# A hybrid encoder layer on one core: weights of the feed-forward in four steps, later gates, and earlier loads for its down projection

## The chip, the cores and the metric

The kernel runs on one core of a Trainium2 chip. The metric is the time of one execution on the device in microseconds (us). The core has a tensor engine (PE) with its weight loads (PEld), a vector engine (DVE), a scalar engine (ACT), GpSimd (POOL) and a queue engine (SP). Each works through its own list of instructions in order, and semaphores hold an instruction until its operands are there. Transfers are issued from SP and POOL and move on their own.

## The reference, cut to what matters

One layer with 1024 positions and a width of 1024, in float32. The change lies in the feed-forward at its end and in the down projection behind it:

```
x  = x + y @ w_out                       # y: the two gated token mixers
h2 = rmsnorm(x, ffn_norm_w)
up = h2 @ ffn_w_up                       # 1024 -> 2 * 2816
gate, val = split(up, 2)
gate = dwconv3(gate, ffn_dw_w) + ffn_dw_b     # along the positions, zero padded
x  = x + (silu(gate) * val) @ ffn_w_down
out = rmsnorm(x, final_norm_w)
```

## The kernel before

Activations lie with channels on the 128 partitions and positions along the free axis, in two halves of 512 positions. Every float32 factor is split into two parts: a high part, which ACT casts to the matmul's reduced type (`A.copy`, line 122), and a low part, which DVE subtracts (line 119). A product then takes three matmuls, high by high, high by low and low by high (`mm3`, lines 144 to 146), each 128x128 by 128x512.

The feed-forward runs over 22 pairs. Pair j makes 128 channels of the gate and 128 of the value, 1024 input channels deep (`ffn_job`, `pair_job`). A pair is a 2x2 block product done with seven block products in place of eight. Products 1, 2, 6, 7, 5, 4 and 3 follow each other on PE; each has four steps of three matmuls, and a job yields after two of those steps, so that a pair has 14 pieces of six matmuls. The weights of the seven products are sums and differences of raw blocks. These sums are made by transfers that add into their target (`G.dma_start(o, a, accum_op=ALU.add)`, line 242), issued from POOL: first the columns `sw` take in the second source, then half of the raw rows `wr` takes in a half of `sw` ("wr<-sw"), then the other half takes in the first ("wr<-wr"). The split of w1 and w2 reads the rows before these adds, the split of w6 and w3 reads them afterwards. w7 and w5 come from `sw` (pages `wq`), w4 from `w4` (page `wq`). There are two buffers for `wr`, one for `sw`, one for `w4`, four pages `wp` (w1/w2 and w6/w3, high and low) and three pages `wq`.

Between the products, ACT copies product 1, the sum after product 6 and product 7 out of PSUM (`copy`, line 270, pages `su`), since product 6 and 5 go on adding in the bank `row`, and product 4 in the bank `col`. DVE forms the four quadrants in `evac` (lines 1278 to 1285). With the last gate quadrant the gate follows: three taps of the convolution (ACT line 1289, then DVE line 1293 twice), Silu (ACT line 1301), times the norm (line 1302), times the value (line 1303), and the store of g to the scratch tensor `d_g` from SP (line 1304), for each half.

The h2 blocks are linear combinations too. Four sets are made while w_out runs (`parts`, with the tile `hx`, and `h7`); the sets for products 4 and 3 are loaded again from scratch (`late_load`, `late_parts`, pages `ft` and `hy`). The norm of h2 is not applied to the activations but to the results: `rstd_over_partitions` sums the squares on PE (line 424), POOL takes the power (lines 408 and 409), and `spread` turns it with PE (line 416) into a row over all partitions (`rs`, line 417).

`run_jobs` prepares a pair's weights when four pieces of the pair before it have been issued; `Stream.fill(n)` issues n pieces. Down (22 blocks of g, in groups of 4, 4, 5, 5 and 4) loads g from `d_g` into `ev` pages (line 1358), splits it into `hx` and `gx` pages, and for each of eight column blocks accumulates a group in PSUM; the first group's results are copied by ACT to `xr` (line 1363), the next groups add there on DVE (line 1369), and the last one adds x2 and goes through the final norm.

The program order is that of the Python code on PE alone (`manual_schedule` for PE). On the other engines, a scheduler at build time orders the instructions by when it takes their operands to be ready. So a cast can stand far ahead of its place in the code.

Of the kernel before, what the change touches and what calls it, by code (L numbers as in the profile page):

```python
# [29 lines left out]
H = 512  # L30
# [15 lines left out]
def tile_hybrid_encoder(  # L46
# [57 lines left out]
    def tmp():  # L104
        return page(mp, "tm", 4)
# [9 lines left out]
        nc.sync.dma_start(t, src)  # L115
        return t

    def split_lo(eng, lo, src, hi):
        eng.tensor_tensor(lo, src, hi.bitcast(F32), op=ALU.subtract)  # L119

    def split(hi, lo, src, eng):
        A.copy(hi, src)  # L122
        split_lo(eng, lo, src, hi)
        return hi, lo

    def w_cols(w, r0, nk, c0, cols=P):
# [12 lines left out]
    def mm3(acc, w, act, k, first, last, again=False):  # L139
# [5 lines left out]
        T.matmul(acc, whi[:, k, :], alo, start=False, stop=False, skip_group_check=again)  # L145
        T.matmul(acc, wlo[:, k, :], ahi, start=False, stop=last, skip_group_check=again)  # L146

    def run_jobs(jobs, lead=0, prime=0):  # L150


        jobs = jobs if isinstance(jobs, collections.deque) else collections.deque(jobs)
        ready = collections.deque()

        def prepare(n):
            while jobs and len(ready) < n:
                prep, run = jobs.popleft()
                ready.append((run, prep()))

        prepare(max(prime, 1))
        if prime:
            yield
        while ready:
            run, w = ready.popleft()
            pieces = run(w)
            for _ in itertools.islice(pieces, lead):
                yield
            prepare(1)
            yield from pieces  # L170
            prepare(1)

    class Stream:
# [48 lines left out]

        return prep, run

    def pair_job(src0, src1, nk, acts, wpool, pool, evac, su=4, first=False):

# [1 line left out]

        def prep():
            def both(src, alt):
                hi, lo = split(w_page(2 * nk, alt), w_page(2 * nk, alt), src, V)
                return [(hi[:, :nk], lo[:, :nk]), (hi[:, nk:], lo[:, nk:])]

            def add(o, a):
                if first:
                    V.tensor_tensor(o, o, a, op=ALU.add)  # L240
                else:
                    G.dma_start(o, a, accum_op=ALU.add)  # L242

            w = {}
# [1026 lines left out]
    def ffn_job(j):  # L1271
        g = gp[j % 2]
        val = [None, None]

        def evac(e, half, x0, x1=None, op=None):
            if e == 1:
                val[half] = page(fu, "ft", 4)
                V.tensor_tensor(val[half], x0, x1, op=op)
                return
            gh = g[:, 1 + half * H : 1 + (half + 1) * H]  # L1280
            if half == 0:
                V.tensor_tensor(gh, x0, x1, op=op)
                return
            V.tensor_tensor(g[:, 1 : 1 + H], g[:, 1 : 1 + H], rstd2[0], op=ALU.mult)
            V.tensor_tensor(gh, x0, rstd2[1], op=ALU.mult)
            for hf in range(2):
                o = hf * H
                c = tmp()
                A.activation(  # L1289
                    c, g[:, o : o + H], AF.Identity, scale=vec("fdw", j), bias=vec("fdb", j)  # L1290
                )
                for k in (1, 2):
                    V.scalar_tensor_tensor(  # L1293
                        c,
                        g[:, o + k : o + k + H],
                        vec("fdw", k * NF + j),
                        c,
                        op0=ALU.mult,
                        op1=ALU.add,
                    )  # L1300
                A.activation(c, c, AF.Silu)
                V.tensor_tensor(c, c, rstd2[hf], op=ALU.mult)
                V.tensor_tensor(val[hf], val[hf], c, op=ALU.mult)
                nc.sync.dma_start(d_g[j][hf], val[hf])

        return pair_job(
            w_cols(ffn_w_up, 0, ND, j * P),
            w_cols(ffn_w_up, 0, ND, DFF + j * P),
            NK2,
            lambda i: h2[i],  # L1310
            fw,
            fu,
            evac,
        )

    s_ffn = Stream(run_jobs([ffn_job(j) for j in range(NF)], 4))
# [4 lines left out]
    s_ffn.fill(5)  # L1321
    rstd2 = [next(st) for st in stats]

    def late_parts(i, src):
        h2[i].append(split(page(fu, "hy", 16, F32R), page(fu, "hy", 16, F32R), src, V))

    def late_load(src):
        t = page(fu, "ft", 4)
        nc.sync.dma_start(t, src)
        return t  # L1330

    for k in range(NK2):
        b21 = late_load(d_t6[k])
        G.dma_start(b21, d_h2[k + NK2][0], accum_op=ALU.add)
        late_parts(4, b21)
    for k in range(NK2):
        late_parts(3, late_load(d_h2[k + NK2][1]))
# [7 lines left out]
    n_g = itertools.cycle([0] * 32 + [1] * 16)  # L1345

# [1 line left out]
        return hx() if next(n_g) == 0 else page(fd, "gx", 16, F32R)  # L1348

    groups = [4, 4, 5, 5, 4]  # L1350
    gs, jobs = [], []

    def load_g(f0, n):
        for f in range(f0, f0 + n):
            gs.append([])
            for half in range(2):
                t = ev()
                nc.sync.dma_start(t, d_g[f][half])
                gs[-1].append(split(g_page(), g_page(), t, V))

    def first_evac(i):
        def f(half, acc):
# [75 lines left out]
    out_sum, out_y = [], []  # L1438
    fnw = fd.tile([P, D], F32, name="fnw")
    f0 = 0  # L1440
    load_g(0, groups[0])
    nc.sync.dma_start(
        fnw, bass.AP(tensor=final_norm_w.tensor, offset=final_norm_w.offset, ap=[[0, P], [1, D]])
    )
    for n, group in enumerate(groups):
        last = n == len(groups) - 1
        for hs in ((0,), (1,)) if last else ((0, 1),):
            st = Stream(run_jobs(down_jobs(f0, group, hs, final_evac if last else add_evac if n else first_evac)))
            st.fill(3)
            while late:  # L1450
                finish(late.pop())
            if not last:
                st.fill(9)
# [3 lines left out]
            st.drain()  # L1457
        f0 += group
    finish(late.pop())
    fd.release()  # L1460
# [32 lines left out]
```

## Time and profile before

| | |
|---|---|
| median of 3 runs | 1862.43 us (1860.35 to 1862.73) |
| profiled execution, its own time | 1861.67 us |
| its span | 1859.9 us |
| granted PE clock, mean | 0.99 |
| DMA queues: from SP, from POOL | 41.5%, 15.2% of 16 engines' span |

The span is the time from the first to the last instruction in the profile; the run's own time has some us around it. "busy" is the time in which an engine works on an instruction; a matmul's end is modelled. In a wait such as "PE mm L144 <- ACT su L270", the tensor engine's matmul of line 144 stood until ACT's instruction of line 270 had written `su`; the numbers are the total, how often, and the longest. In a timeline row, the idle time just before the instruction and what ended it stand in brackets. Rows by stretch give each engine's busy time with its instructions, then the granted clock, the share of busy DMA engines and GB/s. Tiles are called by the program's names without their numbers.

### The profile page before, as it was taken

What the parts mean: (1) busy time and instruction counts of PE and PEld (TensorE: products, weight loads), DVE (VectorE), ACT (ScalarE), POOL (GpSimd) and SP (SyncE); (2) the same over time, 40 slices, a digit from 0 to 9 for tenths busy, and PEclk for the clock granted to TensorE, in tenths of its full rate; (3) what the DMA queues carried; (4) which work ended last, traced back from release to release, by engine and by line L of the source; (5) the groups of instructions that cost most, each with busy time, mean ns of one, the idle gap of its engine ahead of it and who ended that gap; (6) DMA issues with size and microseconds to landing.
All of it is one profiled execution on the core that took longest, in us unless ns stands there. A gap on an engine that the chain in (4) does not pass through costs nothing.

```text
span 1859.9 us, 23747 instructions
## 1 busy us (share of the span) xinstructions
PE 1778.8 (96%) x8574; PEld 1475.4 (79%) x8574; DVE 1275.2 (69%) x1878; ACT 793.9 (43%) x1482; POOL 172.9 (9%) x189
## 2 busy tenths in 40 slices
PE   8989999999999999999989999899999999999996
PEld 6877877887778888888878787677888888788885
DVE  4599999645479999999835565566666767534445
ACT  6443333334555556555442144443343434522124
POOL 1201111111000000000000001211111111000000
PEclk9999999999999999999999999999999999999998
DMA  7657878874753333332238566876676765733135
GB/s 271 215 146 181 180 175 197 198 173 135 222 170 95 109 114 114 110 105 93 73 120 231 182 210 197 177 163 137 149 155 150 151 155 124 218 95 95 56 87 170
DMA packets 324620, 283.51 MB, mean 152 GB/s; under 512 B 14862, under 2 KB 247062, under 8 KB 324502
## 3 DMA queue, kind: packets, MB, share of 16 engines
q1 hardware_dynamic: 273462, 241.10, 41.5%
q0 software_dynamic: 51040, 40.90, 15.2%
q8 instruction: 67, 1.10, 0.2%
q14 instruction: 51, 0.42, 0.1%
HBM read 189.14 MB, written 72.88 MB: 141 GB/s over the span
## 4 chain that ended last, share of the span: by engine, by line
PE 56%; DVE 20%; DMA 13%; ACT 5%; issue 4%; POOL 1%; SPq 0%; DVEq 0%; ACTq 0%; POOLq 0%
PE mm L144 14%; PE mm L145 14%; PE mm L146 13%; DMA tm<-d_a 3%; PE sc L144 3%; PE sc L146 3%; PE sc L145 3%; DVE wp L119 2%; DVE acc L756 2%; DMA wr<-wr 2%; DVE kG L841 2%; DVE DE L841 2%; DVE qF L841 1%; DMA sw<-in_w_in_dram 1%; DMA wr<-sw 1%
## 5 line engine op out<-in xcount | busy, mean ns | idle before, releaser
L144 PE MATMUL mm<-hx,wp 128*128 128x512 f32 x1176 | 477.4, 406 | 19.4 <-DVE ev L541 7.8
L146 PE MATMUL mm<-hx,wp 128*128 128x512 f32 x1176 | 462.5, 393 | 2.9 <-DVE wp L119 2.9
L145 PE MATMUL mm<-hx,wp 128*128 128x512 f32 x1176 | 462.4, 393 | 1.7 <-DVE hx L476 1.7
L122 ACT CAST wp<-wr 128x1024 fp32r<-128x1024 f32 (+2 forms) x193 | 176.6, 915 | 330.2 <-PE mm L145 191.7
L119 DVE TENSOR_TENSOR wp<-wr,wp 128x1024 fp32r<-128x1024 f32 (+2 forms) x193 | 203.5, 1055 | 111.6 <-ACT wp L122 102.0
L144 PEld LDWEIGHTS mm<-hx,wp 128*128 128x128 f32 x1176 | 223.1, 190 | 66.9 <-DVE ev L541 10.3
L146 PEld LDWEIGHTS mm<-hx,wp 128*128 128x128 f32 x1176 | 222.7, 189 | 53.1 <-DVE wp L119 4.6
L145 PEld LDWEIGHTS mm<-hx,wp 128*128 128x128 f32 x1176 | 223.2, 190 | 43.6 <-DVE hx L476 2.0
L756 DVE SCALAR_TENSOR_TENSOR acc<-gl,v_b,acc 128x1024 f32<-128x1024 f32 x120 | 149.4, 1280 | 0.4
L1369 DVE TENSOR_TENSOR xr<-mm,xr 128x512 f32<-128x512 f32 x48 | 33.2, 691 | 80.6 <-PE mm L146 80.6
L949 PE MATMUL sc<-qF,A 128*128 128x128 f32 x512 | 69.2, 279 | 14.0 <-DVE qF L841 13.2
L949 PEld LDWEIGHTS sc<-qF,A 128*128 128x128 f32 x512 | 64.6, 193 | 20.9 <-issue 16.8
L242 POOL DMA_DIRECT2D wr<-sw x38 | 33.7, 887 | 439.8 <-DVE wp L119 176.0
L122 ACT CAST wq<-sw 128x1024 fp32r<-128x1024 f32 x39 | 41.0, 1051 | 75.0 <-PE mm L145 61.0
L946 ACT COPY A<-kG 128x512 f32<-128x512 f32 x64 | 39.6, 618 | 73.5 <-DVE kG L841 51.0
L1293 DVE SCALAR_TENSOR_TENSOR tm<-gp,v_a,tm 128x512 f32<-128x512 f32 x88 | 65.8, 748 | 2.5 <-ACT tm L1289 1.7
L144 PE MATMUL mm<-hy,wp 128*128 128x512 f32 x156 | 61.2, 393 | 1.9 <-ACT su L270 1.9
L144 PE MATMUL tr<-hx,wp 128*128 128x512 f32 x156 | 61.3, 393 | 0.0
L145 PE MATMUL mm<-hy,wp 128*128 128x512 f32 x156 | 61.2, 392 | 0.0
L144 PE MATMUL sc<-hy,wq 128*128 128x512 f32 x156 | 61.1, 392 | 0.0
L146 PE MATMUL sc<-hy,wq 128*128 128x512 f32 x156 | 61.0, 391 | 0.0
L145 PE MATMUL sc<-hy,wq 128*128 128x512 f32 x156 | 60.8, 390 | 0.0
(322 smaller groups left out, 3573.1 us busy)
## 6 DMA issues: line engine op xcount, KB each, us to landing
wr<-in_w_in_dram SPq DMA_DIRECT2D x53, 512.0 KB, 4.9
sw<-in_ffn_w_up_dram SPq DMA_DIRECT2D x44, 256.0 KB, 4.7
sw<-in_ffn_w_up_dram POOLq DMA_DIRECT2D x22, 512.0 KB, 8.7
wr<-in_ffn_w_up_dram SPq DMA_DIRECT2D x22, 512.0 KB, 7.0
d_g<-ft SPq DMA_DIRECT2D x44, 256.0 KB, 3.8
ev<-d_g SPq DMA_DIRECT2D x44, 256.0 KB, 3.4
wr<-sw POOLq DMA_DIRECT2D x38, 256.0 KB, 3.2
wr<-wr POOLq DMA_DIRECT2D x38, 256.0 KB, 4.8
```

The source lines that it names most:

```text
L119: eng.tensor_tensor(lo, src, hi.bitcast(F32), op=ALU.subtract)
L122: A.copy(hi, src)
L144: T.matmul(acc, whi[:, k, :], ahi, start=first, stop=False, skip_group_check=again)
L145: T.matmul(acc, whi[:, k, :], alo, start=False, stop=False, skip_group_check=again)
L146: T.matmul(acc, wlo[:, k, :], ahi, start=False, stop=last, skip_group_check=again)
L242: G.dma_start(o, a, accum_op=ALU.add)
L756: V.scalar_tensor_tensor(acc, g[:, k : k + S], tap(k), acc, op0=ALU.mult, op1=ALU.add)
L841: V.tensor_tensor(o, a, b, op=op)
L946: A.copy(A_t.rearrange("p (b x e) -> p b x e", x=2, e=h), pairs(kG, h))
L949: T.matmul(b[:, c * P : (c + 1) * P].rearrange("p (b x e) -> p b x e", x=2, e=h), A_t[:, c * P : (c + 1) * P], view(qF, c * P, [[2 * h, P ...
L1293: V.scalar_tensor_tensor(c, g[:, o + k : o + k + H], vec("fdw", k * NF + j), c, op0=ALU.mult, op1=ALU.add,)
L1369: V.tensor_tensor(xr[i][half], acc, xr[i][half], op=ALU.add)
```

## The change

- `split` can pin its two instructions (`late=True`): `keep_in_program_order` binds an instruction behind the one that stands before it in the code on its engine.
- The weights of a pair become a generator of steps (`Weights`). Its first step issues the loads and the add into `sw`; the w1/w2 split comes three pieces later, then both adds into `wr`, four pieces on the w7/w5 split, three pieces on w6/w3 and three pieces on w4. In the feed-forward these splits are pinned. The other pairs make all steps at once; both of their adds into `wr` now come before the w7/w5 split in the code.
- `later(n, do)` puts off a piece of code by n pieces. The gates of a pair run three and five pieces into the next pair, with the tap on ACT and the Silu pinned. There are eight `ft` pages in place of four.
- The loads for products 4 and 3 are issued together after three pieces, and split, pinned, some pieces behind.
- The g blocks of down's first group are loaded and split in the last pair of the feed-forward, into `ev` and `tm` pages in turn; in the later groups one half is loaded every two pieces, and split, pinned, four pieces later.

```diff
+    pin = tc.keep_in_program_order
+
+    def split(hi, lo, src, eng, late=False):
+        parts = A.copy(hi, src), eng.tensor_tensor(lo, src, hi.bitcast(F32), op=ALU.subtract)
+        if late:
+            for i in parts:
+                pin(i)
         return hi, lo
...
+    class Weights:
+        def __init__(self, steps):
+            self.parts = {}
+            self.steps, self.wait = steps(self.parts), 0
+            self.tick()
+
+        def tick(self):
+            self.wait -= 1
+            if self.wait <= 0:
+                self.wait = next(self.steps, 1 << 30)
...
-            for _ in itertools.islice(pieces, lead):
-                yield
-            prepare(1)
-            yield from pieces
+            for _ in itertools.islice(pieces, lead):
+                tick()
+                yield
+            prepare(1)
+            for _ in pieces:
+                tick()
+                yield
...
             add(col, raw_w(src1, 2 * nk) if first else src1)
+            yield 3
             w[1], w[2] = both(rows, None)
             add(rows[:, :nk], col[:, nk:])
+            add(rows[:, nk:], rows[:, :nk])
+            yield 4
             w[7], w[5] = both(col, pool)
-            add(rows[:, nk:], rows[:, :nk])
+            yield 3
             w[6], w[3] = both(rows, None)
+            yield 3
             one = w_page(2 * nk, pool)
-            w[4] = split(one[:, :nk], one[:, nk:], a22, V)
-            return w
+            w[4] = split(one[:, :nk], one[:, nk:], a22, V, late)
+
+        def prep():
+            w = Weights(steps)
+            return w if late else w.all()
...
+        def gated(hf):
+            o = hf * H
+            c = tmp()
+            pin(A.activation(c, g[:, o : o + H], AF.Identity, scale=vec("fdw", j), bias=vec("fdb", j)))
+            for k in (1, 2):
+                V.scalar_tensor_tensor(...)
+            pin(A.activation(c, c, AF.Silu))
+            V.tensor_tensor(c, c, rstd2[hf], op=ALU.mult)
+            V.tensor_tensor(val[hf], val[hf], c, op=ALU.mult)
+            nc.sync.dma_start(d_g[j][hf], val[hf])
...
             for hf in range(2):
+                later(3 + 2 * hf, lambda hf=hf: gated(hf))
...
+    s_ffn.fill(1)
+    for k in range(NK2):
+        late_parts(5 + k // 2, 4, d_t6[k], d_h2[k + NK2][0])
+    for k in range(NK2):
+        late_parts(7 + k // 2, 3, d_h2[k + NK2][1])
+    s_ffn.fill(4)
     rstd2 = [next(st) for st in stats]
...
+    landing = itertools.cycle([ev] * 3 + [tmp] * 4)
...
+    s_ffn.fill(14 * (NF - 1) - s_ffn.count)
+    for f in range(groups[0]):
+        for half in range(2):
+            later(4, load_g(f, half))
+            s_ffn.fill(1)
     s_ffn.drain()
+    advance_chores(1 << 10)
...
                 for f in range(f0 + group, f0 + group + groups[n + 1]):
-                    load_g(f, 1)
-                    st.fill(4)
+                    for half in range(2):
+                        later(4, load_g(f, half))
+                        st.fill(2)
```

More of the change, by code (lines that the diff above doesn't have):

```diff
@@ L159, in prepare, with tick @@
                 ready.append((run, prep()))
+                live.append(ready[-1][1])
+        def tick():
+            for w in live:
+                if isinstance(w, Weights):
+                    w.tick()
+            advance_chores()
         prepare(max(prime, 1))
@@ L223, in duo_job, with pair_job, steps @@
         return prep, run
-    def pair_job(src0, src1, nk, acts, wpool, pool, evac, su=4, first=False):
-        def prep():
+    def pair_job(src0, src1, nk, acts, wpool, pool, evac, su=4, first=False, late=False):
+        def steps(w):
             def both(src, alt):
-                hi, lo = split(w_page(2 * nk, alt), w_page(2 * nk, alt), src, V)
+                hi, lo = split(w_page(2 * nk, alt), w_page(2 * nk, alt), src, V, late)
                 return [(hi[:, :nk], lo[:, :nk]), (hi[:, nk:], lo[:, nk:])]
@@ L1286, in evac @@
             for hf in range(2):
[L1287 to L1304, printed above, removed]
+                later(3 + 2 * hf, lambda hf=hf: gated(hf))
         return pair_job(
@@ L1313, in ffn_job @@
             evac,
+            late=True,
         )
@@ L1343, in tile_hybrid_encoder @@
     xr = [[page(fd, "xr", 2 * ND) for _ in range(2)] for _ in range(ND)]
-    n_g = itertools.cycle([0] * 32 + [1] * 16)
-    def g_page():
[L1348 to L1359, printed above, removed]
     def first_evac(i):
@@ L1440, in tile_hybrid_encoder @@
     f0 = 0
-    load_g(0, groups[0])
     nc.sync.dma_start(
```

72 lines of the change are left out of this document (52 added, 20 removed).

## The prediction

> **What bounds the kernel now.** I read the page's busy shares first, then the busy time by stretch, then the tensor engine's own waits.
>
> ```profile
> span 1859.9 us, 23747 instructions
> ...
> PE 1778.8 (96%) x8574; PEld 1475.4 (79%) x8574; DVE 1275.2 (69%) x1878; ACT 793.9 (43%) x1482; POOL 172.9 (9%) x189
> ...
> 1200.00:1300.00 100.00, 96.66 (x419) 78.23 (x418) 64.08 (x85) 39.07 (x55) 17.30 (x16) 1.00 0.68 148
> 1300.00:1400.00 100.00, 100.00 (x436) 81.69 (x435) 66.17 (x88) 40.17 (x56) 16.49 (x15) 1.00 0.71 151
> ...
> 1600.00:1700.00 100.00, 96.83 (x421) 79.73 (x420) 44.17 (x68) 34.65 (x61) 0.00 (x0) 0.98 0.46 140
> ...
> PE sc L416 <- ACT rs L417: 6.1, 1, 6.1
> ...
> PE mm L144 <- ACT su L270: 6.7, 6, 1.6
> ...
> PE mm L144 <- ACT xr L1363: 3.2, 1, 3.2
> ```
>
> PE is 96% busy, and from 1300 on the feed-forward leaves it no idle time. Only small waits can be won: 6.1 us in pair 0 (the spread of the norm behind casts of late loads), 3.3 us in pairs 1 to 5 (100 less 96.66), and 3.2 us where down begins (evacuations behind casts of g). Since PE is full, anything that the change makes later than PE's pace is paid at once, in every one of 22 pairs. So I looked next at what stands just behind PE: the chain that makes the weights of products 6 and 3.
>
> ```profile
> 1344.05 1.05 ACT L122 CAST wp<-wr 128x1024 fp32r<-128x1024 f32 x1 [4.59 <-DMA wr<-wr]
> ...
> 1345.13 1.23 DVE L119 TENSOR_TENSOR wp<-wr,wp 128x1024 fp32r<-128x1024 f32 x1 [2.11 <-ACT wp L122]
> ...
> 1350.90 0.69 DVE L1303 TENSOR_TENSOR ft<-ft,tm 128x512 f32<-128x512 f32 x1
> 1351.50 1.22 DVE L119 TENSOR_TENSOR wp<-wr,wp 128x1024 fp32r<-128x1024 f32 x1
> 1352.64 0.75 DVE L1293 SCALAR_TENSOR_TENSOR tm<-gp,v_a,tm 128x512 f32<-128x512 f32 x1
> ...
> 1353.02 0.89 POOL L242 DMA_DIRECT2D wr<-sw  x1 [7.53 <-DVE wp L119]
> 1356.53 0.84 POOL L242 DMA_DIRECT2D wr<-wr  x1 [2.63 <-DMA wr<-sw]
> ...
> 1361.36 1.05 ACT L122 CAST wp<-wr 128x1024 fp32r<-128x1024 f32 x1 [2.44 <-DMA wr<-wr]
> ...
> 1416.14 0.62 ACT L122 CAST wq<-w 128x512 fp32r<-128x512 f32 x1 [1.94 <-PE sc L146]
> ...
> 1435.42 0.62 ACT L122 CAST wq<-w 128x512 fp32r<-128x512 f32 x1 [1.95 <-PE sc L146]
> ...
> ACT wp L122 <- DMA wr<-wr: 37.3, 10, 4.6
> ```
>
> These are timeline rows (start, length, engine, line, what; most are left out) and, last, ACT's waits from 1310 to 1570. They show a loop. The cast of w6/w3 (1344.05) lets DVE make their low parts (1345.13). DVE is in order, and a few steps later makes the low parts of the next pair's w1/w2 (1351.50). Only then may POOL add into the raw rows that both were read from (1353.02, 3.51 us to the second add at 1356.53). When that has landed, the next w6/w3 are cast (1361.36). One round takes 1361.36 - 1344.05 = 17.31 us. PE takes 1435.42 - 1416.14 = 19.28 us for a pair, so the loop has 2 us to spare, though already in 10 pairs the cast waits last for that transfer.
>
> **The change part by part.** The order built for the changed kernel is the same as before on every engine up to the last w_out outputs, the moved adds of the w_in pairs too, and on PE it is the same to the end. All that moves is casts, gates and loads of the last two stages.
>
> *Gates later, casts pinned: the loop.* A cast held in program order now pins its low part on DVE too. In the built order DVE has, from low w6/w3 on: low w4, both taps of gate 0, the evacuation of product 2, gate 0's multiply by the norm, the norm of the next gate's first half, gate 0's product, both taps of gate 1, its multiply and product, and only then low w1/w2. Each gate's multiply waits for a Silu on ACT between. Before, the Silus were long done or hidden, and one gate's taps lay ahead of the loop. These prices hold from 1310 to 1570:
>
> ```profile
> L1293 DVE SCALAR_TENSOR_TENSOR tm<-gp,v_a,tm 128x512 f32<-128x512 f32 x53 | 39.6, 748 | 0.5
> ...
> L119 DVE TENSOR_TENSOR wq<-w,wq 128x512 fp32r<-128x512 f32 x13 | 9.0, 692 | 0.1
> ...
> L1301 ACT ACTIVATE tm<-tm 128x512 f32<-128x512 f32 x27 | 16.9, 627 | 29.7 <-DVE tm L1293 29.7
> ...
> 1376.47 0.85 POOL L242 DMA_DIRECT2D wr<-wr  x1 [2.60 <-DMA wr<-sw]
> ...
> 1380.83 1.05 ACT L122 CAST wp<-wr 128x1024 fp32r<-128x1024 f32 x1 [2.62 <-DMA wr<-wr]
> ...
> 1435.02 0.85 POOL L242 DMA_DIRECT2D wr<-wr  x1 [2.63 <-DMA wr<-sw]
> ...
> 1440.47 1.05 ACT L122 CAST wp<-wr 128x1024 fp32r<-128x1024 f32 x1 [4.42 <-DMA wr<-wr]
> ```
>
> Back to back, a 512-wide DVE step costs 0.60 us (1350.90 to 1351.50) and a 1024-wide one 1.14 (1351.50 to 1352.64). From the cast of w6/w3: 1.08 to its low part; 1.14 for that; 0.61 low w4; 1.50 two taps, each needing the one before (2 x 0.748); 0.70 through Silu and back (0.627 and two handovers; the evacuation of product 2 hides here); 1.82 for three steps; 1.50 taps; 0.70 Silu, with nothing to hide it; 1.21 two steps; 1.22 low w1/w2. Sum 11.48. Then 0.30 to POOL (1352.72 to 1353.02), 3.51 to the second add, and from there to the cast 4.36 at least (1376.47 to 1380.83) and 5.45 at most (1435.02 to 1440.47); I take the middle, 4.9. The round becomes 20.2 us (19.65 to 20.74). That is 0.92 us over PE's 19.28 (0.37 to 1.46). It is the old round plus 2.9: the w4 step, two more taps, one and a half bare Silus. From pair 1 to pair 21 there are 20 rounds: 18.4 us (7.4 to 29.2). The first rounds use up some slack: product 6 needs its low part 0.46 us after it starts, 5.5 us into the pair, so a cast 3.6 us into the pair costs nothing; it comes about 2.3 in (product 4 ends at 1435.4, product 3 takes twelve matmuls like product 1, 2.72 from 1150.56 to 1153.28, the pair begins at 1438.1, the cast at 1440.47). That takes 1.3 off. The 3.3 us of waits in pairs 1 to 5 are absorbed (the copy of product 1 now follows the cast at once): -3.3. Together +13.8.
>
> *Weights of pair 0 cast late: the start.*
>
> ```profile
> 1139.65 1.05 ACT L122 CAST wp<-wr 128x1024 fp32r<-128x1024 f32 x1 [2.24 <-PE mm L145]
> ...
> 1152.02 0.71 ACT L1228 ACTIVATE xq<-x,v_a 128x512 f32<-128x512 f32 x1
> ...
> 1150.56 0.39 PE L144 MATMUL mm<-hx,wp 128*128 128x512 f32 x1
> ...
> 1153.28 1.84 PE L424 MATMUL sc<-ones_m,rs 128*128 128x1 f32 x16
> 1154.98 0.49 PE L144 MATMUL tr<-hx,wp 128*128 128x512 f32 x1
> ...
> 1161.48 2.68 POOL L1334 DMA_DIRECT2D ft<-d_h  x3 [3.19 <-DMA ft<-d_t]
> ...
> 1170.90 2.07 PE L416 MATMUL sc<-tm,ones_m 128*128 128x512 f32 x2 [6.09 <-ACT rs L417]
> 1171.99 1.42 PE L144 MATMUL sc<-h,wq 128*128 128x512 f32 x1
> 1173.20 0.63 PE L145 MATMUL sc<-h,wq 128*128 128x512 f32 x1
> ```
>
> Before, w1/w2 of pair 0 were cast at 1139.65, and PE began product 1 the moment w_out ended (1150.56). Now that cast is pinned behind the last three casts of h2, which need the last xq (done 1152.73), then three subtractions of 0.60: ACT is free at 1155.4, w1/w2 are high at 1156.45 and low, behind three other low parts, at 1157.75. PE stands about 5.9 us. After a wait of that length (6.09 before 1170.90) the next matmuls start 1.09, 1.21 and 0.43 us apart instead of 0.50, 0.23 and 0.23: 1.8 us more. Product 1 ends about 1161.3 in place of 1153.28: 8.0 late. Behind it come the sums (1.70) and product 2 (2.73), to 1165.7. The raw rows can be added to only after 1157.75; 0.30 + 3.51 later, with POOL's three adds for the late h2 pieces ahead (2.68), the second add goes out near 1162 and w6/w3 are cast 4.9 to 7 later. PE waits again some 3.3 us, and 1.6 for its clock: 4.9. The second spread waits 0.95 behind a cast. Against this 1.7 (first copy), 6.6 (second spread) and 1.8 (its cold matmuls) are gone. Net 8.0 + 4.9 + 0.95 - 10.1 = +3.75; bounds 1 (the second wait hidden) and 7 (cast at 1169.5). I take 3.5.
>
> [...]
>
> *The g loads in the last pair.*
>
> ```profile
> 1592.19 0.39 PE L144 MATMUL mm<-hx,wp 128*128 128x512 f32 x1
> ...
> 1600.14 0.39 PE L146 MATMUL mm<-hx,wp 128*128 128x512 f32 x1
> 1603.70 0.71 PE L144 MATMUL mm<-hx,wp 128*128 128x512 f32 x1 [3.17 <-ACT xr L1363]
> 1604.21 0.63 PE L145 MATMUL mm<-hx,wp 128*128 128x512 f32 x1
> ```
>
> Down began at 1592.19 and stood 3.2 us from 1600.14; then matmuls 0.43 to 0.5 apart, 1.7 us lost. With the first casts in the last pair that 4.9 goes. New waits come: SP's queue puts the seventh g load behind the store of the last but one gate, so its low part is ready about 1 us after PE asks for it; and the last pair's two gates, pinned, stand ahead of the first xr copies, so that the fourth bank is late by about 1.7 us. I take -2.2 (bounds -4.9 and 0).
>
> *At nothing:* the eight late h2 loads go out in one run ahead of pair 1's columns, which lie a pair ahead; the raw rows pass w4's load on SP, both a pair ahead; g loads by half pieces in the later groups are cast 5 us after their issue, and the add into xr has three banks. Each would cost under 1 us a place without that cover.
>
> Sum: +13.8 + 3.5 - 2.2 = +15.1 on the profiled run's 1861.67 us (span 1859.9 and 1.8 around it), which is 0.8 below the median 1862.43. That gives 1876.8, so 1877.
>
> **The rivals.** *The loop stays shorter than PE's pace.* It decides at 0.92 us less than my sum: Silus hidden better, or landings at 4 us. For it: 2 us of slack today. Against: the low part of w1/w2 follows a Silu that nothing hides. PE then sets the pace: +3.5 - 3.3 - 4.9 = -4.7, so 1857, faster. *The loop only just passes*, with landings at the lowest row: 7.4 in place of 18.4, so 1866. *The loop is longer*: landings at 5.45 or more, since the first add now meets the store of the gate just finished, +10.8, and the down start gains nothing, +2.2: 1890 and up.
>
> **How the numbers follow.** Forecast (1869 to 1886) 0.60, just passing 0.10, longer 0.12, shorter 0.18. About 0.2% (3.7 us) is what a measurement can tell from no change: the shorter loop holds 0.14 of faster and 0.04 of the same; just passing gives 0.05 to the same. Faster 0.14, same 0.09, slower 0.77. The range runs from 1861 to 1893; it leaves out the clearly faster case and the tail of the longer one.
>
> **What would show it.** Right: between 1220 and 1600 PE waits in nearly every pair, about 1 us, at the first matmul of product 6 or its third, for ACT or DVE at the wp split; pairs 20.2 us apart; POOL's first add 11.8 us after the w6/w3 cast, released by DVE; a wait near 6 us where the feed-forward begins, and none for the spread; down's 3.2 us gone or shared out. Wrong: pairs 19.3 us apart with PE full, or PE waiting for another tile, such as the copy of product 7, which a pinned Silu now precedes.

## The result, and the profile after

The changed kernel takes 1907.55 us (median of 4 runs, 1903.69 to 1907.70) beside 1861.39 us for the kernel before on the same chip (4 runs, 1855.49 to 1862.73): a ratio of 1.0249, 95% interval 1.0223 to 1.0275. It is slower, as forecast, by three times what was forecast (46 us, not 15), and outside the range. The profiled execution has a span of 1905.7 us, 45.8 over that of before.

The page of the changed kernel, TensorE's waits over the whole span, and the busy time by stretch (length, PE, PEld, DVE, ACT and POOL busy with instructions, granted clock, DMA share, GB/s):

```profile
span 1905.7 us, 23648 instructions
...
PE 1801.2 (95%) x8574; PEld 1480.3 (78%) x8574; DVE 1274.4 (67%) x1878; ACT 788.7 (41%) x1482; POOL 172.3 (9%) x189
...
PE mm L146 <- ACT su L330: 25.3, 16, 2.9
PE mm L146 <- ACT wp L122: 14.0, 3, 6.3
...
1200.00:1300.00 100.00, 94.45 (x391) 74.77 (x390) 61.43 (x82) 37.17 (x52) 14.20 (x13) 0.97 0.65 142
1300.00:1400.00 100.00, 93.67 (x394) 74.06 (x393) 58.99 (x80) 36.71 (x53) 15.78 (x14) 0.98 0.64 137
...
1600.00:1700.00 100.00, 99.95 (x439) 81.79 (x438) 51.37 (x75) 40.17 (x68) 4.21 (x4) 1.00 0.47 132
```

From 1200 to 1600 PE no longer is full. It stands for the copy of product 1 (`su`), and the matmul count of a stretch, the better measure, falls from 436 to 394. No wait for `xr` is left.

PE also ran slow behind many of these waits. The granted clock fell to 0.50 six times between 1222 and 1591, for 3.41 us each, behind waits of 1.80 to 2.90 us. The first such stretch, the one right after it, and the last one (columns as above):

```profile
1222.41:1225.82 3.41, 3.38 (x8) 2.63 (x9) 3.36 (x5) 1.79 (x4) 0.68 (x1) 0.50 0.60 69
1225.82:1229.23 3.41, 3.41 (x16) 2.75 (x16) 3.22 (x5) 2.29 (x4) 0.00 (x0) 1.00 1.27 243
1587.63:1591.04 3.41, 3.41 (x9) 2.67 (x8) 3.28 (x6) 1.43 (x3) 0.00 (x0) 0.50 1.12 135
```

Eight or nine matmuls start in a slow stretch, sixteen in the full one. So the listed waits for `su`, 22.4 us from 1180 on, are not all that PE loses there: six times half of 3.41 us, about 10 us, went to the slow clock, an estimate from these rows.

One round of the changed kernel, on the timeline (start, length, engine, line, what; the bracket is the idle time before and what ended it):

```profile
1412.41 1.05 ACT L122 CAST wp<-wr 128x1024 fp32r<-128x1024 f32 x1 [8.42 <-DMA wr<-wr]
1413.37 0.58 ACT L330 COPY su<-mm 128x512 f32<-128x512 f32 x1
1413.50 1.23 DVE L122 TENSOR_TENSOR wp<-wr,wp 128x1024 fp32r<-128x1024 f32 x1 [4.18 <-ACT wp L122]
...
1416.81 0.63 ACT L1348 ACTIVATE tm<-tm 128x512 f32<-128x512 f32 x1 [1.63 <-DVE tm L1340]
...
1420.86 0.63 ACT L1348 ACTIVATE tm<-tm 128x512 f32<-128x512 f32 x1 [1.29 <-DVE tm L1340]
...
1422.25 0.69 DVE L1350 TENSOR_TENSOR ft<-ft,tm 128x512 f32<-128x512 f32 x1
1422.86 1.22 DVE L122 TENSOR_TENSOR wp<-wr,wp 128x1024 fp32r<-128x1024 f32 x1
...
1424.61 0.90 POOL L296 DMA_DIRECT2D wr<-sw  x1 [10.31 <-DVE wp L122]
1428.16 0.86 POOL L296 DMA_DIRECT2D wr<-wr  x1 [2.65 <-DMA wr<-sw]
1433.59 1.04 ACT L122 CAST wp<-wr 128x1024 fp32r<-128x1024 f32 x1 [9.73 <-DMA wr<-wr]
...
1435.17 0.50 PE L146 MATMUL mm<-hx,wp 128*128 128x512 f32 x1 [1.26 <-ACT su L330]
```

This is the loop: cast of w6/w3 (1412.41), its low part (1413.50), both gates with their two Silus, low part of the next w1/w2 (1422.86, done 1424.08), first add (1424.61), second add (1428.16), next cast (1433.59). The copy of product 1 stands behind that cast on ACT, and PE's product 6 stands behind the copy. PE is not a link of it: from the cast to the low part's end VectorE takes 11.65 to 11.72 us in each of the eighteen rounds, whether PE's clock has fallen or not. These rounds, from the cast at 1220.85 to the one at 1606.16, take 385.31 us, 21.41 each.

The start of the feed-forward, TensorE, POOL and ACT, and two stretches behind its waits:

```profile
1152.32 0.39 PE L148 MATMUL mm<-mg,wp 128*128 128x512 f32 x1
1158.42 0.80 PE L146 MATMUL mm<-hx,wp 128*128 128x512 f32 x1 [5.71 <-ACT wp L122]
...
1160.01 0.88 POOL L296 DMA_DIRECT2D wr<-sw  x1 [7.05 <-DMA ft<-d_t]
1161.53 2.58 POOL L1388 DMA_DIRECT2D ft<-d_h  x3 [0.64 <-DMA ft<-d_t]
1167.96 0.85 POOL L296 DMA_DIRECT2D wr<-wr  x1 [3.85 <-DMA wr<-sw]
...
1174.21 1.04 ACT L122 CAST wp<-wr 128x1024 fp32r<-128x1024 f32 x1 [1.54 <-DMA wr<-wr]
1175.31 0.80 PE L146 MATMUL mm<-hx,wp 128*128 128x512 f32 x1 [6.34 <-ACT wp L122]
...
1158.40:1164.20 5.80, 5.66 (x13) 3.97 (x14) 1.31 (x2) 0.00 (x0) 3.46 (x4) 0.50 0.93 279
...
1175.30:1181.00 5.70, 5.65 (x12) 3.97 (x13) 1.21 (x1) 1.14 (x4) 1.62 (x1) 0.50 0.59 124
...
1641.08 0.39 PE L148 MATMUL mm<-hy,wp 128*128 128x512 f32 x1
```

There are two waits, 5.71 and 6.34 us, and after each the clock was 0.50 for all twelve matmuls of the product: 5.8 and 5.7 us, where twelve at a clock of 1.00 take 2.72 (1150.56 to 1153.28 in the kernel before). The first add, among the transfers of the late h2 parts, needs 7.95 us until the second can go out (1160.01 to 1167.96).

Where the 45.8 us are. The last matmul of w_out starts 2.0 us later than before (1152.32, 1150.33), ahead of everything whose order the change moves; it lies between 1145.5 and 1153.6 in the thirteen profiles. Pair 0 ends at 1194.95 (before 1182.91), which is 12.0, so 10.0 for the start. The last pair ends at about 1641.3 (1592.19), so pairs 1 to 21 take 446.4 us for 409.3: 37.1. The rest, -3.3, is the down part. 2.0 + 10.0 + 37.1 - 3.3 = 45.8.

### The profile page after: what moved, and what is told of

Same layout as the page of the kernel before. It is cut to its first block, busy times and chain, and to the rows that moved or that the text cites. A ratio compares the mean times of both kernels' runs of the same rounds, so it can differ in the third digit from the quotient of the medians.

```text
span 1905.7 us, 23648 instructions
## 1 busy us (share of the span) xinstructions
PE 1801.2 (95%) x8574; PEld 1480.3 (78%) x8574; DVE 1274.4 (67%) x1878; ACT 788.7 (41%) x1482; POOL 172.3 (9%) x189
## 4 chain that ended last, share of the span: by engine, by line
PE 32%; DVE 29%; DMA 20%; issue 11%; ACT 6%; POOL 1%; SPq 0%; ACTq 0%; POOLq 0%; DVEq 0%
PE mm L146 8%; PE mm L147 8%; PE mm L148 8%; DMA wr<-wr 6%; DMA wr<-sw 5%; DVE wp L122 4%; DVE acc L816 4%; DMA tm<-d_a 3%; DMA sw<-in_w_in_dram 2%; DVE tm L1340 2%; DVE kG L901 2%; DVE qF L901 2%; DVE DE L901 2%; ACT wp L122 1%; DMA wr<-in_w_in_dram 1%
## 5 line engine op out<-in xcount | busy, mean ns | idle before, releaser
L146 PE MATMUL mm<-hx,wp 128*128 128x512 f32 x1176 | 484.4, 412 | 46.5 <-ACT su L330 22.4
L148 PE MATMUL mm<-hx,wp 128*128 128x512 f32 x1176 | 469.6, 399 | 3.0 <-DVE wp L122 2.2
L147 PE MATMUL mm<-hx,wp 128*128 128x512 f32 x1176 | 467.9, 398 | 1.2 <-DVE hx L536 1.2
L146 PEld LDWEIGHTS mm<-hx,wp 128*128 128x128 f32 x1176 | 225.8, 192 | 99.4 <-ACT su L330 29.1
L148 PEld LDWEIGHTS mm<-hx,wp 128*128 128x128 f32 x1176 | 225.8, 192 | 62.5 <-DVE wp L122 13.7
L147 PEld LDWEIGHTS mm<-hx,wp 128*128 128x128 f32 x1176 | 226.4, 193 | 43.8 <-DVE hx L536 1.7
L330 ACT COPY su<-mm 128x512 f32<-128x512 f32 x78 | 45.2, 579 | 48.0 <-PE mm L148 46.9
L146 PE MATMUL sc<-hy,wq 128*128 128x512 f32 x156 | 61.1, 391 | 0.0
L148 PE MATMUL sc<-hy,wq 128*128 128x512 f32 x156 | 61.0, 391 | 0.0
```

The source lines that it names most:

```text
L146: T.matmul(acc, whi[:, k, :], ahi, start=first, stop=False, skip_group_check=again)
L330: A.copy(t, acc)
```

## The experiments

TensorE, VectorE and ScalarE are PE, DVE and ACT of the profile. The same measure is used for all: the feed-forward's length, from the start of w_out's last matmul to that of the last pair's last one. It is 441.6 us in the kernel before (1150.33 to 1591.97) and 488.8 in the changed one (1152.32 to 1641.08). Each time is given beside the kernel before on the same chip, which differs from chip to chip (1857.9, 1864.1 and 1865.3 in the three sets below).

**Does VectorE's pinned low part make the loop?** First the pin on it is taken away, for a pair's weights alone:

```diff
         if late:
-            for i in parts:
-                pin(i)
+            pin(parts[0])
+        if late is True:
+            pin(parts[1])
...
-            late=True,
+            late=1,
```

> The changed kernel, but only the ScalarE cast of a pair's weights is held in program order; VectorE's low part (the subtraction) may go where the order built for the kernel puts it, which is ahead of the second gate's last products. Theory (the round is a loop: cast w6/w3, VectorE's queue up to the low part of w1/w2, two accumulating transfers, next cast): some 5 us less stand in VectorE's queue between the low parts of w6/w3 and w1/w2, so cast to cast could take 18.3 us, less than TensorE's 19.28; the +37 of the loop go, the +10 of the start and the -3 of the down part stay: 1870 us (1866 to 1877), TensorE's waits on su copies nearly gone. Rival (the accumulating transfers are slower in the new order, whatever VectorE does): stays at 1895 to 1908. Rival (the held cast on ScalarE is the wait): stays near 1907.

Measured 1863.89 us beside 1857.90, ratio 1.0036 (1.002 to 1.0051). The length is 448.6. TensorE's waits and two stretches of this kernel:

```profile
PE mm L147 <- ACT wp L122: 14.7, 3, 7.1
...
PE mm L147 <- ACT su L331: 3.1, 3, 1.4
...
1300.00:1400.00 100.00, 100.00 (x437) 81.83 (x436) 69.48 (x93) 42.23 (x59) 16.67 (x15) 1.00 0.73 155
1400.00:1500.00 100.00, 100.00 (x437) 81.75 (x436) 67.51 (x89) 40.41 (x58) 16.89 (x16) 1.00 0.69 150
```

With ScalarE's cast still held, PE is full again and the loop's loss gone; the start's waits stay (5.71 and 7.08). From the cast to the low part's end it takes 9.69 us on average in place of 11.66: 2 us less, not the 5 expected, but enough. Neither the transfers nor the hold on ScalarE were the cause. The second run keeps every pin, and lets the gates come after that low part:

```diff
-                later(3 + 2 * hf, lambda hf=hf: gated(hf))
+                later((7 if j < NF - 2 else 3) + 2 * hf, lambda hf=hf: gated(hf))
```

> The changed kernel, but the two gates of a pair are issued four pieces later (7 and 9 instead of 3 and 5), except in the last two pairs, so that the held low part of w1/w2 stands in front of both gates; everything stays held. Theory (loop through VectorE's queue): low parts of w6/w3 and w4, two results of product 2, low part of w1/w2 are some 4.7 us instead of 11.7, so the round falls under TensorE's 19.28: 1870 us (1866 to 1880). Rival (holding on either engine is itself the cost, or the transfers are slower): 1895 to 1908.

Measured 1871.60 beside 1857.90, ratio 1.0083 (1.0055 to 1.011). The length is 455.4; the waits for `su` from 1180 on fall from 22.4 us to 3.8, and PE is nearly full (98.7 to 99.4% busy from 1200 to 1600). So the gates' place before the low part is what fills the loop. Two further runs change the content of VectorE's queue by a known step. One adds a step in front of the low part:

```diff
             V.tensor_tensor(c, c, rstd2[hf], op=ALU.mult)
+            if hf:
+                V.tensor_scalar_mul(c, c, 1.0)
```

> The changed kernel with one VectorE operation more per pair (the second gate's 128x512 result multiplied by 1.0 in place), ahead of the held low part of w1/w2. Theory (loop through VectorE's queue, TensorE waits for it): each 128x512 step of VectorE in front of that low part costs its own 0.6 us in each of 20 rounds: 12 us (8 to 15) more than the changed kernel, so 58 us over the kernel before; rounds of 22.0. Rival (VectorE has slack and the round is set by the transfers or by ScalarE): 0 to 2 us more.

Measured 1916.20 beside 1864.10, ratio 1.0285 (1.0251 to 1.0319). That is 52.1 us over the kernel before where the changed kernel has 46.2, so 5.9 more and not 8 to 15, with intervals that overlap; the trace is sharper. Timeline of this kernel:

```profile
1420.61 0.43 DVE L1351 TENSOR_SCALAR tm<-tm 128x512 f32<-128x512 f32 x1
1421.07 0.69 DVE L1352 TENSOR_TENSOR ft<-ft,tm 128x512 f32<-128x512 f32 x1
...
1421.68 1.22 DVE L122 TENSOR_TENSOR wp<-wr,wp 128x1024 fp32r<-128x1024 f32 x1
...
1423.43 0.89 POOL L296 DMA_DIRECT2D wr<-sw  x1 [10.45 <-DVE wp L122]
```

The step costs 0.46 us (1420.61 to 1421.07; I had taken 0.6), and 20 rounds of it are 9.2. The length grows by 9.7, to 498.5, and the round from 21.41 to 21.92. VectorE has no slack ahead of this low part. The other run takes time out, by letting ACT's two gate steps go where the built order puts them:

```diff
-            pin(A.activation(c, g[:, o : o + H], AF.Identity, ...))
+            A.activation(c, g[:, o : o + H], AF.Identity, ...)
...
-            pin(A.activation(c, c, AF.Silu))
+            A.activation(c, c, AF.Silu)
```

> The changed kernel, but the two ScalarE steps of each gate (the Identity and the Silu) are not held in program order; the casts and low parts of the weights stay held. In the built order both Identity steps and the Silu come earlier, one tap stands ahead of the low part of w6/w3, so VectorE doesn't wait for the two Silu between the low parts of w6/w3 and w1/w2. Theory (loop through VectorE's queue): 11.67 us from cast to the low part's end become some 10.3, the round 20.0 instead of 21.4 and TensorE still waits: 25 to 30 us less than the changed kernel, some 18 us over the kernel before. Rival (the round is the transfers'): 0 to 5 us less. Rival (holding the gates on ScalarE is the whole loss): the time of the kernel before plus the start's 10.

Measured 1888.64 beside 1864.10, ratio 1.0143 (1.011 to 1.0177): 25 us over the kernel before, where 18 were expected. The round is 20.35, the length 469.6. Timeline of this kernel:

```profile
1404.55 1.05 ACT L122 CAST wp<-wr 128x1024 fp32r<-128x1024 f32 x1 [7.42 <-PE mm L148]
...
1412.97 0.75 DVE L1340 SCALAR_TENSOR_TENSOR tm<-gp,v_a,tm 128x512 f32<-128x512 f32 x1 [0.29 <-ACT tm L1338]
...
1413.31 1.05 ACT L122 CAST wp<-wr 128x1024 fp32r<-128x1024 f32 x1
...
1414.38 1.23 DVE L122 TENSOR_TENSOR wp<-wr,wp 128x1024 fp32r<-128x1024 f32 x1 [0.66 <-DMA w<-in_ffn_w_up_dram]
...
1415.91 0.90 POOL L296 DMA_DIRECT2D wr<-sw  x1 [9.16 <-DMA w<-in_ffn_w_up_dram]
```

From cast to the low part's end VectorE takes 11.06 us on average over the rounds, not the 10.3 expected: the next gate's first tap now stands ahead of the low part, and that tap waits for its ACT step; the low part then waits for its own cast, which stands on ACT behind that step (1413.31, ended at 1414.36). The round follows the queues again. The brackets of three of these rows name other releasers. But the second add, issued at 1399.09, landed about 0.1 us before the cast at 1404.55, and POOL's add follows the end of the low part by 0.29 or 0.30 us in 17 of 19 rounds, so the loop is still closed by them.

**Do the stores lengthen the adds?** The first add is longer than 3.55 us in one round of three. A gate's store is the neighbour that comes to mind:

```diff
-            V.tensor_tensor(val[hf], val[hf], c, op=ALU.mult)
-            nc.sync.dma_start(d_g[j][hf], val[hf])
+            V.tensor_tensor(c, val[hf], c, op=ALU.mult)
...
                 V.tensor_tensor(val[half], x0, x1, op=op)
+                nc.sync.dma_start(d_g[j][half], val[half])
                 return
```

> The changed kernel, but the store of a gate's half is issued when its value half is made, before the gate multiplies it, so no 256 KB store stands beside the first accumulating transfer; the gate's last product goes to a scratch tile. Left out: what is stored is the value half without its gate. Theory (loop set by VectorE's queue; the store's contention is the part of the first add above 3.5 us, mean 3.8 with 4.2 to 5.3 in each third round): rounds of 21.4 become 21.0 to 21.2, 4 to 8 us less than the changed kernel. Rival (contention of the two transfers is what makes the loop longer than TensorE's pace): rounds of 20 or less, 25 us or more less. If the time doesn't move, the third rounds' longer add is not the store's.

Measured 1915.22 beside 1864.10, ratio 1.0283 (1.0253 to 1.0313), a miss: the length rose to 498.7 and the round to 21.96. The edit did not do what the expectation says. The value half is made on VectorE right behind the low part, so its store went out exactly beside the first add. That add's mean rose from 3.85 to 4.34 us, the round by 0.55. So a 256 KB store beside an add costs it about half a microsecond on average, but each third round is longer than its neighbours here too (5.48 to 5.85 us), though every round has the same stores. What these rounds have is in the changed kernel's DMA view from the first add's issue to the second's, first a round of 3.55 us (1424.61 to 1428.16), then one of 4.23 (1445.78 to 1450.01):

```profile
q0 software_dynamic: 144, 0.26, 40.7%
q1 hardware_dynamic: 1, 0.00, 0.0%
```

```profile
q0 software_dynamic: 144, 0.26, 34.8%
q8 instruction: 1, 0.02, 1.6%
q1 hardware_dynamic: 1, 0.00, 0.0%
```

The add is the same 144 packets, and of SP's queue there is one packet: no store stands beside it. In the long round one packet of a queue that the view calls instruction (q8), 0.02 MB, runs beside them. All of the long rounds from 1300 to 1600 (4.23 to 5.30 us, five of them) have that packet, and none of the others (3.49 to 3.55). The packet starts 1.1 to 1.7 us behind the add's issue. Two of the short rounds have a smaller packet of another such queue (q14, 0.01 MB) in the add's first 0.2 us. The kernel before, too, has the 0.02 MB packet beside adds of this loop: 0.71 and 0.55 us behind the issue of two that took 4.27 and 4.14 us (1236.65, 1563.43), and 3.32 us behind the issue of one that took 3.51 (1411.79). So the packet beside an add is not enough; when it comes seems to matter.

**The start.** Pair 0's weights are made in one step, unpinned, the others as changed:

```diff
-            late=True,
+            late=j > 0,
```

> The changed kernel, but the weights of pair 0 are made in one step, not held, as in the kernel before; pairs 1 to 20 as changed. Theory (start and loop are two separate losses that add): the start's +10 go, the round of 21.4 us stays: 1897 us (1894 to 1900), rounds of pair 2 to 20 still 21.4. Rival (the loop makes the pace from its first cast on, and the start's lateness is hidden in it, or pair 1's adds are late anyway): 1903 to 1908.

Measured 1895.18 beside 1857.90, ratio 1.0204 (1.0178 to 1.0229). The length is 478.6, so 10.2 less than changed, as much as the start's whole loss (10.0); the rounds take 21.18. That the two agree is partly luck. Pair 0 takes 37.0 us here (42.6 in the changed kernel, 32.6 before), so 5.6 come from the start; the other 4.5 come behind it, from pairs 1 to 21 (441.9 in place of 446.4), most of them from the first round, 21.5 us in place of 25.9. The loop stays without the start's loss, but the two are not wholly separate. TensorE's waits of this kernel over its whole span:

```profile
PE mm L146 <- ACT su L330: 25.8, 20, 2.5
...
PE mm L146 <- ACT hy L122: 6.5, 1, 6.5
```

The 6.5 us stand before the third step of pair 0's product 3 (1182.18), now early enough to wait for the late h2 parts; in the kernel before, the spread stood 6.1 us nearby. To see why the second wait of the start was 6.3 and not 3.3, the late h2 parts were put two pieces later:

```diff
-    s_ffn.fill(1)
+    s_ffn.fill(3)
     for k in range(NK2):
-        late_parts(5 + k // 2, 4, d_t6[k], d_h2[k + NK2][0])
+        late_parts(3 + k // 2, 4, d_t6[k], d_h2[k + NK2][0])
     for k in range(NK2):
-        late_parts(7 + k // 2, 3, d_h2[k + NK2][1])
+        late_parts(5 + k // 2, 3, d_h2[k + NK2][1])
-    s_ffn.fill(4)
+    s_ffn.fill(2)
```

> The changed kernel, but the eight loads and four accumulating transfers of the late h2 parts are issued two pieces later, behind the first accumulating transfer of pair 0's weights, as in the kernel before; their splits stay held at the same pieces. Theory (the first add took 7.7 us to land because it shares the engines with these transfers): TensorE's second wait at the start falls from 6.3 to some 3 us, 3 to 4 us less than the changed kernel, loop unchanged. Rival (the second wait is the held cast's place on ScalarE alone, the transfer's length does not matter), or the h2 parts then land late and the wait moves to product 4: no change (within 1.5 us).

Measured 1902.97 beside 1864.10, ratio 1.0223 (1.019 to 1.0256); the length is 487.8 and the second wait 6.25. This tells nothing: in the built order these transfers kept their places on both queues, since a later place in the code holds nothing back there. So they were pinned:

```diff
-        nc.sync.dma_start(t, src)
+        pin(nc.sync.dma_start(t, src))
         if more is not None:
-            G.dma_start(t, more, accum_op=ALU.add)
+            pin(G.dma_start(t, more, accum_op=ALU.add))
```

> The changed kernel, but the loads and accumulating transfers of the late h2 parts are themselves held in program order, so that on their queues they stand behind both accumulating transfers of pair 0's weights (the run with them two pieces later had left their place on the queues as it was). Theory (the first add's 7.7 us to landing is shared bandwidth with these 2 MB and the adds): the first add lands in 3.5 to 5 us, TensorE's second wait falls from 6.3 to 3 us or less; a wait for the late parts, of 3 to 8 us, comes at product 4 in its place, so the time is 1900 to 1910. Rival (the add is slow there for another reason, the first transfer after a long rest of its queue): landing stays 7 us or more and the second wait 6.

Measured 1912.07 beside 1865.32, ratio 1.0261 (1.0231 to 1.029). Timeline of this kernel:

```profile
1157.17 0.88 POOL L296 DMA_DIRECT2D wr<-sw  x1 [7.05 <-DVE wp L122]
1160.71 0.83 POOL L296 DMA_DIRECT2D wr<-wr  x1 [2.66 <-DMA wr<-sw]
...
1167.15 0.51 PE L148 MATMUL mm<-hx,wp 128*128 128x512 f32 x1 [1.36 <-DVE wp L122]
...
1185.38 0.79 PE L146 MATMUL sc<-hy,wq 128*128 128x512 f32 x1 [7.41 <-ACT hy L122]
```

Without the late parts beside it, the first add is through in 3.54 us instead of 7.95, and the second wait is 1.36 instead of 6.34; the h2 parts then come late by 7.4. So the 7.95 come from the transfers beside it. In the changed kernel's DMA view from 1160.01 to 1167.96 the engines are busy throughout, most of it for SP's queue:

```profile
q1 hardware_dynamic: 1059, 1.90, 73.9%
q0 software_dynamic: 222, 0.42, 28.7%
```

**The down part alone, and both repairs.** The kernel before with only the g loads in the last pair and the half steps in the later groups:

```diff
+    s_ffn.fill(14 * (NF - 1) - s_ffn.count)
+    for f in range(groups[0]):
+        for half in range(2):
+            later(4, load_g(f, half))
+            s_ffn.fill(1)
     s_ffn.drain()
```

> The kernel before, with one part of the change alone: the first g loads and their splits are issued in the last pair of the feed-forward part, and later groups in two half steps; weights, gates and late h2 parts as before. Theory: the wait of 3.2 us at the start of the down part goes and nothing else moves: 1858 us (1856 to 1860) beside 1861.4. Rival (the loads come against the last pair's weights or stores): 1861 to 1866, with the wait moved into the feed-forward part's end.

Measured 1855.53 beside 1857.90, ratio 0.999 (0.9971 to 1.0008): a gain of the expected size, but no difference that the times prove. The trace shows no wait of PE from 1587 to 1640, where the kernel before stands 3.2 us for `xr`, and a length of 440.9. Last, the unpinned low part, pair 0 early (both diffs above), and all else as changed:

> Both repairs together: only the ScalarE cast of a pair's weights is held, and pair 0's weights are made in one step, not held; the gates, the h2 parts and the g loads as in the changed kernel. Theory (start, loop and down part are separate and add): the feed-forward part some 439 us against 441.6 in the kernel before (su waits of the loop gone, the start's wait on the late h2 parts of 6.5 us in place of the rstd wait of 6.1), the down part's 3.2 us gone: 4 to 7 us under the kernel before, ratio 0.996 to 0.998. Rival (the start's loss returns with the loop's pace): 0 to 4 us over.

Measured 1860.14 beside 1865.32 (12 and 23 runs), ratio 0.9982 (0.9969 to 0.9996): slightly faster than the kernel before, by 5.2 us in the medians and 3.4 by the ratio, so at the edge of what was expected, and some 2.6% under the changed kernel by the two ratios. The length is 442.4, not the 439 expected and no shorter than before, so the gain is the down part's (263.5 us behind the last pair's last matmul, 267.9 in the kernel before). A stretch of its loop:

```profile
1300.00:1400.00 100.00, 100.00 (x438) 81.70 (x437) 65.42 (x87) 38.97 (x55) 17.34 (x16) 1.00 0.70 151
```

The same with the splits of the late h2 parts unpinned as well:

```diff
-            h2[i].append(split(*pages, t, V, True))
+            h2[i].append(split(*pages, t, V))
```

> As the run before, but the splits of the late h2 parts are not held either. Theory (TensorE's wait of 6.5 us at pair 0's product 4 is for the accumulating transfers of these parts, not for the place of their casts): within 1.5 us of the run before. Rival (the hold is the wait): 3 to 6 us less than the run before.

Measured 1862.56 beside 1865.32, ratio 0.9982 (0.9966 to 0.9998): the same ratio as the run before, 2.4 us more by the medians. The waits on `hy` (3.7 us) are gone, but 5.0 us for the spread have come back, the same trade as between the kernel before and the run with pair 0 early. So the time came out as the theory had it, and its reason did not. The wait is at product 3, whose parts have no accumulating transfer, and not at product 4. And part of it was the hold's: the matmul that stood 3.2 us in the run before starts 30.4 us behind w_out's last one without the hold, 31.7 with it.

## Why the prediction was right in kind and wrong in size

**The loop: right mechanism, round too short.** That the pinned low part behind both gates closes a loop longer than PE's pace is shown from both sides: without the pin PE is full, with the gates behind it nearly so; a step added or taken moves the round with it. One link was different: the prediction looked for PE's wait at the cast's own pages (`wp`) and took a wait for another tile as a sign against it. PE waits for the copy of product 1 (`su`), which ACT makes behind the same cast, in 13 of the 21 pairs. The loop is the one forecast, its last step towards PE is not. The size failed in the sum of the round, 20.2 forecast and 21.41 measured. Means over those eighteen rounds, term by term:

| term | forecast | measured |
|---|---|---|
| cast to end of the low part of w1/w2 | 11.48 | 11.66 |
| VectorE to POOL | 0.30 | 0.57 |
| first add to second add | 3.51 | 3.85 |
| second add to next cast | 4.9 | 5.33 |
| sum | 20.2 | 21.41 |

The mis-sized step is this sum: all four terms were too low, most of all the second add to the next cast (by 0.43), the first add (0.34) and VectorE to POOL (0.27). VectorE to POOL came from one row; it was 0.53 or 0.54 in 17 of the 18 rounds and 1.16 in one. The first add came from one row too; it was 3.53 on average in 13 rounds and 4.69 in the five with the instruction packet. In the kernel before, the second add to the cast has a mean of 5.10 in the 15 rounds of the same stretch that wait for its landing (4.36 to 5.46); the middle of two rows, 4.9, was below it. PE's own pace is subtracted, so a sum short by 1.2 of 21.4 made the excess 0.9 instead of 2.1, and 20 rounds multiply that. The miss here is 23.3 us (37.1 against 13.8). Eighteen rounds by 1.21 are 21.8 of it; the first round, 25.9 us long, adds 5.7, and the last, 19.0, takes 1.2 off. Two errors the other way take off 3.1: the first cast led by more than was counted, 3.2 us in place of 1.3 (it stands where pair 1 begins, at 1194.92, and the last one 3.2 us into its pair), and the kernel before lost 4.4 us in pairs 1 to 21, not 3.3 (409.3 less 21 by 19.28). The rival of a longer loop had the landings right (5.33 beside its 5.45), but blamed the gate's store for the first add. No store stands beside it; what the long rounds show there is the packet of the instruction queue.

**The start: two terms too small.** Of +10.0 against +3.5, the first wait was right (5.71, forecast 5.9). The second was 6.34 in place of 3.3, because the late h2 loads, which the prediction costed at nothing, share the DMA engines with the first add (3.54 alone, 7.95 beside them). And the slow clock behind the two waits was priced at 1.8 us, from one row, and at 1.6, an estimate that no run shows; it cost 3.1 (5.78 less 2.72) and 3.0 (5.69 less 2.72). Behind the 3.17 us before 1603.70 the kernel before lost 1.7 us, with the clock at 0.50 for 3.41 us. (Its 8.0 us for product 1 is also 0.3 more than the 5.9 and 1.8 that it names.)

The length of the slow stretch varied between the profiled executions. Behind waits of 5.7 to 7.7 us PE worked at 0.50 for 2.8 us in the kernel before and for all twelve matmuls of the product here, twice; in the run with the gates after, the matmuls stood 0.43 us apart in place of 0.23 for 3.8 and 3.5 us. In the profile of the kernel before and in that of the changed one, all changes of the granted clock lie 3.41 us or a multiple of it apart, to within 0.02 us. In the kernel before it fell at 1166.91, inside the wait, and rose two steps later at 1173.74, so that only 2.8 us of work were slow; in the changed kernel it was 0.50 from 1157.55 for 6.83 us and from 1171.21 for 10.24. A step of 3.41 us at 0.50 loses 1.7 us if PE works throughout, an estimate from these rows, and the 3.1 and 3.0 lie between one such step and two.

**The down part: right in size.** Forecast -2.2 (0 to -4.9), measured -3.3; alone, it takes its wait away without a new one. The two new waits in the forecast did not come, here either: PE is 99.95% busy from 1600 to 1700. Without them the sum would have been -4.9, so that -2.2 came near is partly luck. Why it is 3.3 and not 4.9 stays open; this part differs between runs with the g loads early (262.9 to 265.7 us).

**What was not in the sum:** 2.0 us upstream of the change, within what the runs of the kernel before differ by. Then the misses are 23.3 + 6.5 + 2.0 - 1.1 = 30.7, and 15.1 + 30.7 = 45.8.

## What to carry to other kernels

Where a change closes a loop a little longer than the bound, its excess is the difference of two large numbers: take each term as a mean over many rounds, and let the range follow the excess times the rounds. Even that would not have been enough here: with the means of the kernel before, 3.66 for the first add and 5.10 for the second, the sum is 20.5, since each term is 0.18 to 0.27 us longer in the changed kernel. A pin holds an instruction behind everything queued before it on its engine (cast to the low part's end: 11.66 us with the low part pinned, 9.69 without), so pin the one that has to be late (the cast) and leave free the one that releases a transfer (the low part). Loads that are hidden as far as their own use goes can still take bandwidth from a short transfer on the path: the first add took 7.95 us beside the late h2 loads, 3.54 without.

## What the runs showed of the hardware that was not expected

- One packet of an instruction queue (0.02 MB) beside a 256 KB accumulating transfer: 4.23 to 5.30 us from add to add instead of 3.49 to 3.55. That the one delays the other is read from their coming together in five rounds of five, with the packet 1.1 to 1.7 us behind the add's issue; in the kernel before, adds with the packet 0.71, 0.55 and 3.32 us behind their issue took 4.27, 4.14 and 3.51 us. It was not tried alone, and what the packet carries is not shown.
- The same transfer took 7.95 us beside the late h2 loads and adds, and 3.54 without them. A 256 KB store issued beside it made its mean 4.34 instead of 3.85.
- From the end of a VectorE step to the POOL transfer that it releases it took 0.53 or 0.54 us in 17 of 18 rounds of the changed kernel, 0.29 or 0.30 in 17 of 19 with the gates' ACT steps unpinned. Why it differs stays open.
- In the loop of the changed kernel the granted clock fell to 0.50 six times, for 3.41 us each, behind waits of 1.80 to 2.90 us; a wait of 2.00 us before 1328.92 left it at 1.00. Counted in steps of 3.41 us from one change of the clock, each fall stands at the end of a step in which PE had stood for 1.84 us or more; in no other step of this loop did it stand for more than 1.30. This is read from one trace, not tried.
